# Output projection, first 1024 columns: seven products of block sums for six attention heads' K-tiles

## The chip, the cores and the metric

The kernel runs on one core of a Trainium2 chip. The metric is the device time of one execution in microseconds, the median of several runs. All times inside an execution are counted from the start of the profiled span. The profile page names the engines: PE is the matrix engine (PEld its weight load), DVE the vector engine, ACT the scalar engine, POOL the general engine that here only starts a few loads and does a few small operations, and SP the queue that starts the loads of weights.

## The reference

One decoder layer on 256 tokens of width 2048, in float32:

```python
h = rms_norm(x, ln_mix_pre[l])
proj = h @ w_in[l]
q, k, v, z, xbc, dt_raw = jnp.split(proj, splits, axis=-1)
attn = moba_attention(q.reshape(shp), k.reshape(shp), v.reshape(shp), rel_bias)
ssm = mamba2_mixer(z, xbc, dt_raw, ssm_conv_w[l], ...)
mixed = jnp.concatenate([attn, ssm], axis=-1) @ w_out[l]
x = x + rms_norm(mixed, ln_mix_post[l])
h = rms_norm(x, ln_ffn_pre[l])
u = causal_depthwise_conv(h @ w_ffn_up[l], ffn_conv_w[l], ffn_conv_b[l])
gate, up = jnp.split(u, [FFN_HIDDEN], axis=-1)
f = (jax.nn.gelu(gate, approximate=True) * up) @ w_ffn_down[l]
x = x + rms_norm(f, ln_ffn_post[l])
```

The change is in the line of `mixed`: a product of 256 x 2048 by 2048 x 2048. Attention has 8 heads of width 128, so one head is one K-tile of 128 rows of `w_out`; the other 8 K-tiles come from the state-space half.

## The kernel before

**Precision.** Each float32 operand is kept as two float32r summands, `hi` (rounded) and `lo` (the rest), and a product is three matmuls: hi by hi, hi by lo of the weights, lo by hi. The activations of the output projection lie in `mT`, sixteen K-tiles by two summands by 256 tokens.

**Weights.** All weights pass through one stream, the class `Weights`. A unit is 512 KB, 128 x 1024 floats. For a plain unit SP starts the load into `raw`, ACT writes `whi` and DVE writes `wlo`:

```python
self.load(out=raw[:, s], in_=self.units[i][0][:, s])          # L85, SP
nc.scalar.copy(hi[:, s], raw[:, s])                           # L86, ACT
nc.vector.tensor_tensor(lo[:, s], raw[:, s], f32(hi[:, s]),   # L87, DVE
                        op=ALU.subtract)
```

There are four buffers each of `raw`, `whi` and `wlo`. Loads go in order, and the load of a unit waits until the `wlo` of the unit four places earlier is written. After each unit that PE has used, `tick` fetches the next one and counts down the list of deferred work. `deepen` (after the mixer's buffers are given back) adds three buffers to `whi` and to `wlo`, none to `raw`, and lets the next three ticks fetch two units each.

**Pairs.** The down projection of the feed-forward half already has units of another kind, written `Q` in its orders (`FIVE`, `FOUR`): two units of weights (`same` and `other`) make four steps on PE. The third step's weights (`two`) and the fourth's (`more`) are sums that DVE forms from the two loaded ones (L141, L144, L145, into a tile `ts`). Each of the four gets its own `whi` (L137, ACT) and `wlo` (L146, DVE). PE multiplies them by block sums of the activations (`quad_operands`, L1075 to L1089) in `product` (L1095 to L1097): seven products for a 2 x 2 block of the result where plain units take eight. `quad_sums` (L1104 to L1108) adds them up.

**Output projection.** Its 2048 columns are four chunks of 512. A chunk has 8 units (two K-tiles by 512 columns each); a unit is 12 matmuls of 128 x 512: two token tiles, two K-tiles, three matmuls (L317 to L319, `rows_part`). Each chunk has two PSUM tiles `pa`, one for each token tile, from a pool of four, so chunk 2 takes over the two tiles of chunk 0. Chunks 0 and 1 are opened with the four units of the state-space half each, while the last attention heads are still being finished by deferred work on the same engines (`logits`, `transposed`, `values`). Then the mixer's buffers are given back, and POOL starts four loads of 1 MB for what follows: two halves of `xt`, `wpost` and `lnrow` (L821, L826, L829). ACT scales `wpost` once (L827). Then come the four attention units of chunk 0 and those of chunk 1, chunk 2 with eight units and chunk 3.

When a chunk is complete, `post` runs for each token tile: ACT sums the squares out of PSUM (L235), DVE multiplies by `wpost` into `mm` (L850) and that by `lnrow` (L842). With L850 done the PSUM tile is free. Six products of `xt` by `lnrow` (L845) are deferred by 9 to 14 ticks.

**Order.** The instructions of the engines are put in order by a scheduler with its own estimate of durations, when the program is built; on the chip each engine takes its instructions in that order, and an instruction whose input is late holds up those behind it on its engine.

Of the kernel before, what the change touches and what calls it, by code (L numbers as in the profile page):

```python
# [158 lines left out]


@with_exitstack
def decoder_layer(ctx, tc, x, xT, win, wdt, wout, wup, wdown, relb, vec, cols, mconv, fconv,
# [248 lines left out]
    with ExitStack() as mctx:  # L411
        mx = mctx.enter_context(tc.tile_pool(name="mx", bufs=1))
        mT = mx.tile([P, KT, 2, S], F32R, name="mT")

# [432 lines left out]
        def post(c):  # L847
            def fn(t, ps):
                square_sum(ss[0][t][:, c:c + 1], ps)
                nc.vector.tensor_tensor(mm[:, t, chunk(c)], ps, wpost[:, chunk(c)], op=ALU.mult)  # L850
# [221 lines left out]

    def quad_operands(k, cg, cu):
# [10 lines left out]
        nc.vector.tensor_tensor(v[:, 4:8:2], v[:, 0:2], v[:, 3::-3], op=ALU.subtract)  # L1084
        nc.vector.tensor_tensor(v[:, 5], v[:, 4], v[:, 1], op=ALU.subtract)
        nc.vector.tensor_tensor(v[:, 7], v[:, 2], v[:, 5], op=ALU.add)
        src, hi, lo = g8[0][:, P:], gx[:, j, 0, :], gx[:, j, 1, :]
        nc.scalar.copy(hi, src)
        nc.vector.tensor_tensor(lo, src, f32(hi), op=ALU.subtract)  # L1089
# [306 lines left out]
```

## Time and profile before

| what | value |
|---|---|
| median of 3 runs | 1097.23 us (1096.92 to 1097.73) |
| the profiled execution | 1097.02 us, span 1095.2 us |
| mean granted PE clock | 0.999 |
| PE, PEld, DVE, ACT, POOL busy | 1089.5, 936.1, 885.4, 622.8, 14.5 us |
| first matmul of the output projection | 277.41 us |
| first matmul of chunk 2 | 323.90 us |
| loads of `w_out` | 32 of 512 KB, median 4.0 us to landing |
| POOL's loads after the mixer | 4 of 1 MB, started from 297.24 to 298.89 us |

The busy shares are means over the layer. What the change touches lies between 277 and 324 us, and in that stretch each engine is read by itself: when a `whi` or a `wlo` is written, and when PE asks for it. In a timeline row the columns are start, duration, engine, line, operation, output from input, count, and in brackets the idle time before it and what ended it.

### The profile page before, as it was taken

The page shows a single profiled execution, that of the slowest core. Times are in us where ns is not written, and L with a number is a line of the kernel's source. Part 1 is how long each engine was busy: PE and PEld are TensorE (multiplying, and loading weights), DVE is VectorE, ACT ScalarE, POOL GpSimd, SP SyncE. Part 2 cuts the span into 40 slices and gives each one's busy share as a digit, 9 for nine tenths or more (in the row PEclk, how much of TensorE's full clock was granted, in tenths as well). Part 3 has the DMA queues.
Part 4 walks back from the last instruction along what each step waited for, and adds up shares of the span by engine and source line. Part 5 has one row for each costly group of instructions (what it writes and reads, how often), then busy time and mean ns, then how long its engine had stood idle before and what let it go on. Part 6 is the DMA issues. An engine that isn't in the chain of part 4 may idle for free.

```text
span 1095.2 us, 15949 instructions
## 1 busy us (share of the span) xinstructions
PE 1089.5 (99%) x5858; PEld 936.1 (85%) x5858; DVE 885.4 (81%) x1422; ACT 622.8 (57%) x945; POOL 14.5 (1%) x24
## 2 busy tenths in 40 slices
PE   9999999999999999999999999999999999999998
PEld 7888888888888998888888888888888888888887
DVE  6689976766568699888878999978888787888987
ACT  6666544644455486655555564646556555565552
POOL 0000000000000000000000000000000000000000
PEclk9999999999999999999999999999999999999999
DMA  9858544554687276656665476675566665656562
GB/s 308 301 174 269 191 154 152 177 180 166 182 320 252 76 254 212 208 183 192 190 191 191 135 232 190 215 245 186 187 189 193 189 192 193 189 178 217 185 219 88
DMA packets 61646, 217.59 MB, mean 199 GB/s; under 512 B 7104, under 2 KB 8912, under 8 KB 60928
## 3 DMA queue, kind: packets, MB, share of 16 engines
q1 hardware_dynamic: 59616, 207.53, 58.5%
q0 software_dynamic: 1664, 8.59, 2.1%
q8 instruction: 46, 0.75, 0.3%
q10 hardware_dynamic: 288, 0.46, 0.1%
q14 instruction: 32, 0.26, 0.1%
HBM read 214.44 MB, written 2.11 MB: 198 GB/s over the span
## 4 chain that ended last, share of the span: by engine, by line
PE 99%; DMA 0%; SPq 0%; ACT 0%; DVE 0%; issue 0%
PE pa L253 37%; PE pa L254 19%; PE pa L317 5%; PE pa L319 5%; PE pa L318 5%; PE ph L318 4%; PE ph L317 4%; PE ph L319 4%; PE pa L1096 1%; PE pa L1097 1%; PE pa L1095 1%; PE pab L253 1%; PE ph L1096 1%; PE ph L1097 1%; PE ph L1095 1%; PE pa L262 1%
## 5 line engine op out<-in xcount | busy, mean ns | idle before, releaser
L86 ACT CAST whi<-raw 128x1024 fp32r<-128x1024 f32 (+2 forms) x353 | 365.2, 1038 | 323.0 <-PE pa L253 186.6
L87 DVE TENSOR_TENSOR wlo<-raw,whi 128x1024 fp32r<-128x1024 f32 (+2 forms) x353 | 424.7, 1208 | 141.6 <-ACT whi L86 133.6
L253 PE MATMUL pa<-h,whi 128*128 128x512 f32 x1360 | 471.7, 394 | 0.0
L254 PE MATMUL pa<-h,wlo 128*128 128x256 f32 x1360 | 379.2, 279 | 0.0
L253 PEld LDWEIGHTS pa<-h,whi 128*128 128x128 f32 x1360 | 255.4, 188 | 57.5
L254 PEld LDWEIGHTS pa<-h,wlo 128*128 128x128 f32 x1360 | 255.3, 188 | 0.0
L253 PE MATMUL pa<-hT,whi 128*128 128x512 f32 x384 | 137.0, 398 | 0.0
L254 PE MATMUL pa<-hT,wlo 128*128 128x256 f32 x384 | 107.2, 280 | 0.0
L253 PEld LDWEIGHTS pa<-hT,whi 128*128 128x128 f32 x384 | 72.1, 188 | 15.8 <-issue 0.2
L1034 DVE SCALAR_TENSOR_TENSOR cfc<-cfu,fcv,cfc 128x255 f32<-128x255 f32 (+1 forms) x176 | 83.4, 479 | 2.1 <-ACT cfc L1032 0.6
L317 PE MATMUL ph<-whi,gT 128*128 128x512 f32 x190 | 73.9, 389 | 0.0
L319 PE MATMUL ph<-whi,gT 128*128 128x512 f32 x190 | 73.9, 389 | 0.0
L318 PE MATMUL ph<-wlo,gT 128*128 128x512 f32 x190 | 73.9, 389 | 0.0
L254 PEld LDWEIGHTS pa<-hT,wlo 128*128 128x128 f32 x384 | 72.2, 188 | 0.4 <-issue 0.2
L137 ACT CAST whi<-ts 128x1024 fp32r<-128x1024 f32 x36 | 37.3, 1049 | 31.3 <-DVE ts L145 16.8
L1032 ACT ACTIVATE cfc<-cfu,fcv 128x256 f32<-128x256 f32 x88 | 52.2, 598 | 3.7 <-DVE cfu L1031 3.7
L317 PE MATMUL pa<-whi,hT 128*128 128x512 f32 x128 | 51.1, 399 | 0.0
L317 PE MATMUL pa<-whi,mT 128*128 128x512 f32 x128 | 50.3, 393 | 0.0
L319 PE MATMUL pa<-whi,hT 128*128 128x512 f32 x128 | 50.1, 391 | 0.0
L318 PE MATMUL pa<-wlo,hT 128*128 128x512 f32 x128 | 50.0, 391 | 0.0
L318 PE MATMUL pa<-wlo,mT 128*128 128x512 f32 x128 | 50.0, 390 | 0.0
L319 PE MATMUL pa<-whi,mT 128*128 128x512 f32 x128 | 49.9, 390 | 0.0
(306 smaller groups left out, 1391.2 us busy)
## 6 DMA issues: line engine op xcount, KB each, us to landing
raw<-in_wup_dram SPq DMA_DIRECT2D x176, 512.0 KB, 3.5
raw<-in_wdown_dram SPq DMA_DIRECT2D x88, 512.0 KB, 3.9
raw<-in_win_dram SPq DMA_DIRECT2D x85, 512.0 KB, 3.6
...
xt<-in_x_dram POOLq DMA_DIRECT2D x2, 1024.0 KB, 7.2
...
```

Source lines behind the costliest of these rows:

```text
L86: nc.scalar.copy(hi[:, s], raw[:, s])
L87: return lambda: nc.vector.tensor_tensor(lo[:, s], raw[:, s], f32(hi[:, s]), op=ALU.subtract)
L137: nc.scalar.copy(hi[:, :n], raw[:, :n])
L253: nc.tensor.matmul(ps, w[0][:, s], both, start=(k == 0), stop=False)
L254: end[0] = nc.tensor.matmul(ps[:, c], w[1][:, s], hi, start=False, stop=(k == KT - 1)).ins
L317: nc.tensor.matmul(ps, a, w[0][:, s], start=(first and j == 0), stop=False)
L318: nc.tensor.matmul(ps, a, w[1][:, s], start=False, stop=False)
L319: end[0] = nc.tensor.matmul(ps, b, w[0][:, s], start=False, stop=(last and j == 1)).ins
L1032: nc.scalar.activation(c, u, AF.Identity, scale=wv[:, 2:3], bias=wv[:, 3:4])
L1034: nc.vector.scalar_tensor_tensor(c[:, sh:], u[:, :S - sh], wv[:, 2 - sh:3 - sh], c[:, sh:], op0=ALU.mult, op1=ALU.add)
L1095: nc.tensor.matmul(ps, a, w[0][:, s], start=first, stop=False)
L1096: nc.tensor.matmul(ps, a, w[1][:, s], start=False, stop=False)
```

## The change

Three of the four attention units of chunk 0 and the three of chunk 1 with the same K-tiles (heads 0 to 5) become three pairs; one pair covers two heads and both chunks. Heads 6 and 7 stay plain. The order of the first 1024 columns is the string `OUTER`: four units of chunk 0, two of chunk 1, and then, after the mixer's buffers are given back, pair, unit of chunk 1, pair, unit of chunk 1, pair, unit of chunk 0, unit of chunk 1.

- The weights' sums use the free half of `mm` instead of `ts` (class `Spare`).
- When a head's values come out of PSUM, ACT also copies them to `og`; after each second head DVE forms the block sums (`block_sums`) and ACT and DVE split the four new blocks into `oq`.
- A pair's seven products go to four PSUM tiles `pm7` of their own and to three of the four chunk tiles. After the third pair `first_sums` writes them into `mm`: one copy on ACT, four operations on DVE.
- `post` of chunks 0 and 1 now first adds PSUM to `mm` on DVE; the sum of squares and the product by `wpost` read `mm`. With that addition done the PSUM tile is free.
- The products of `xt` by `lnrow` are deferred by 17 to 22 ticks. The units of `w_out` stand in the new order in memory.
- In the feed-forward half the same operations as before are now called through the shared helpers.

```diff
+OUTER = "000011Q1Q1Q01"
+OQ = OUTER.count("Q")
...
+class Spare:
...
+    def tile(self, *args, **kwargs):
+        self.n += 1
+        return self.places[self.n % len(self.places)]
...
+    def block_sums(v):
...
+        nc.vector.tensor_tensor(v[:, 4:8:2], v[:, 0:2], v[:, 3::-3], op=ALU.subtract)
+        nc.vector.tensor_tensor(v[:, 5], v[:, 4], v[:, 1], op=ALU.subtract)
+        nc.vector.tensor_tensor(v[:, 7], v[:, 2], v[:, 5], op=ALU.add)
+
+    def split(hi, lo, src):
+
+        nc.scalar.copy(hi, src)
+        nc.vector.tensor_tensor(lo, src, f32(hi), op=ALU.subtract)
+
+    def product_of(ps, a, b, w, h, first, last):
+
+        s = chunk(h)
+        nc.tensor.matmul(ps, a, w[0][:, s], start=first, stop=False)
+        nc.tensor.matmul(ps, a, w[1][:, s], start=False, stop=False)
+        end[0] = nc.tensor.matmul(ps, b, w[0][:, s], start=False, stop=last).ins
+
+    def first_sums(f, p1, p6, p7, q5):
+
+        tt = nc.vector.tensor_tensor
+        nc.scalar.copy(f[0][0], p1)
+        tt(f[1][0], p6, f[0][0], op=ALU.add)
+        tt(f[0][1], p7, f[1][0], op=ALU.add)
+        tt(f[1][1], q5, f[0][1], op=ALU.subtract)
+        tt(f[1][0], q5, f[1][0], op=ALU.subtract)
...
+    def out_units():
+
+        found, at = [], 0
+        for what in OUTER:
+            if what == "Q":
+                found += [("same", wout[at]), ("other", wout[at + 1]), ("two",), ("more",)]
+                at += 2
+            else:
+                found += units(wout, at, 1)
+                at += 1
+        return found + units(wout, at, 16)
...
+                if h < 2 * OQ:
+                    out_operands(h, po[:, S - 1::-1])
...
+            def out_operands(h, a):
+
+                j, odd = divmod(h, 2)
+                if not odd:
+                    og[0] = ax.tile([P, 8 * P], F32, name="og", tag="og", bufs=1)
+                    nc.scalar.copy(blocks(og[0])[:, 1::-1], blocks(a))
+                    return
+                nc.scalar.copy(blocks(og[0])[:, 2:4], blocks(a))
+                block_sums(blocks(og[0]))
+                split(oq[:, j, 0, :], oq[:, j, 1, :], og[0][:, 4 * P:])
...
+            mm = pers.tile([P, NT, D], F32, name="mm", tag="mm", bufs=1)
+            ws.sums = Spare([mm[:, t, UE:] for t in range(NT)])
             lo, hi = range(8, KT, 2), range(0, 8, 2)
             first = [chunk_psums() for _ in range(2)]
-            for c in range(2):
-                rows_chunk(first[c], mT, lo, last=False)
+            taken = [list(lo) + list(hi[OQ:]) for _ in range(2)]
+            for what in OUTER[:6]:
+                c = int(what)
+                rows_step(first[c], mT, taken[c].pop(0), first=len(taken[c]) == 4 - OQ + 3)
...
             def fn(t, ps):
+                m = mm[:, t, chunk(c)]
+                if c < 2:
+                    nc.vector.tensor_tensor(m, ps, m, op=ALU.add)
+                    ps = m
                 square_sum(ss[0][t][:, c:c + 1], ps)
-                nc.vector.tensor_tensor(mm[:, t, chunk(c)], ps, wpost[:, chunk(c)], op=ALU.mult)
+                nc.vector.tensor_tensor(m, ps, wpost[:, chunk(c)], op=ALU.mult)
...
+        def out_pair():
...
+            once = [psum("pm7") for _ in range(4)]
+            p1, p7, q5, p6 = once
+            j = 0
+            for what in OUTER[6:]:
+                if what == "Q":
+                    for items in (((p1, 0, 0), (first[1][0], 6, 1)), ((first[0][0], 1, 0),),
+                                  ((q5, 3, 0), (p7, 5, 1)), ((p6, 4, 0), (first[0][1], 2, 1))):
+                        w = ws.take()
+                        for ps, block, h in items:
+                            mine = any(ps is z for z in once)
+                            out_product(ps, j, block, w, h, mine and j == 0,
+                                        mine and j == OQ - 1)
+                        tick()
+                    j += 1
+                    if j == OQ:
+                        first_sums([[mm[:, t, chunk(n)] for t in range(NT)] for n in range(2)],
+                                   p1, p6, p7, q5)
+                else:
+                    c = int(what)
+                    k = taken[c].pop(0)
+                    rows_step(first[c], mT, k, last=not taken[c],
+                              soon=None if taken[c] else post(c))
...
-            defer(9 + i, x_weighted, t, c)
-        for c in range(2):
-            rows_chunk(first[c], mT, hi, first=False, soon=post(c))
+            defer(17 + i, x_weighted, t, c)
+        out_pair()
```

The scheduler's order around it, at the places where PE's weights come from. First ACT, from the stretch in which POOL's four loads are under way to the end of the first two chunks. Before: the units 10 to 17 of `w_out` (`raw_2998` is unit 10, `raw_3016` unit 11, `raw_3067` unit 12, and so on).

```order
L86 CAST whi_3068<-raw_3067 128x1024
L86 CAST whi_2999<-raw_2998 128x1024
L86 CAST whi_3074<-raw_3073 128x1024
L86 CAST whi_3017<-raw_3016 128x1024
L86 CAST whi_3092<-raw_3091 128x1024
L86 CAST whi_3098<-raw_3097 128x1024
L86 CAST whi_3116<-raw_3115 128x1024
L827 ACTIVATE wpost_3038<-wpost_3038 128x2048
L86 CAST whi_3122<-raw_3121 128x1024
```

And now. `raw_3091` is load 11 (a plain unit of chunk 1), `raw_3105` and `raw_3123` are loads 12 and 13, the third pair's `same` and `other`; `raw_3153` and `raw_3165` are loads 14 and 15, the plain units behind that pair; `whi_3134` and `whi_3143` are the third pair's `two` and `more`, `pm7_3043` one of its products.

```order
L88 CAST whi_3092<-raw_3091 128x1024
L139 CAST whi_3103<-raw_3105 128x1024
L139 CAST whi_3121<-raw_3123 128x512
L88 CAST whi_3154<-raw_3153 128x1024
L912 ACTIVATE wpost_3026<-wpost_3026 128x2048
L139 CAST whi_3134<-mm_2862 128x1024
L88 CAST whi_3166<-raw_3165 128x1024
L387 COPY mm_2862<-pm7_3043 128x512
L139 CAST whi_3143<-mm_2862 128x1024
L88 CAST whi_3184<-raw_3183 128x1024
```

The weights of load 14 and the scaling of `wpost` now stand ahead of the third pair's `two`, which PE uses before load 14; load 15 and the copy stand ahead of `more`.

Second DVE, from the third pair's `two` to the operation that frees the PSUM tile of chunk 0's first token tile, which chunk 2 takes over (`pa_2863` in the rows of the change). Before, from the last `wlo` ahead of it (`raw_3121` is unit 17, two units into chunk 2):

```order
L87 TENSOR_TENSOR wlo_3099<-raw_3097,whi_3098 128x1024
L87 TENSOR_TENSOR wlo_3117<-raw_3115,whi_3116 128x1024
L845 TENSOR_TENSOR xl0_3044<-xt_3025,lnrow_3041 128x512
L87 TENSOR_TENSOR wlo_3123<-raw_3121,whi_3122 128x1024
L850 TENSOR_TENSOR mm_3024<-pa_2837,wpost_3038 128x512
L850 TENSOR_TENSOR mm_3024<-pa_2838,wpost_3038 128x512
```

And now (`raw_3183` is load 16, chunk 2's first unit; `raw_3204`, `raw_3216` and `raw_3228` are loads 18 to 20):

```order
L89 TENSOR_TENSOR wlo_3167<-raw_3165,whi_3166 128x1024
L148 TENSOR_TENSOR wlo_3144<-mm_2862,whi_3143 128x1024
L89 TENSOR_TENSOR wlo_3185<-raw_3183,whi_3184 128x1024
L89 TENSOR_TENSOR wlo_3197<-raw_3195,whi_3196 128x1024
L388 TENSOR_TENSOR mm_2862<-pm7_3046,mm_2862 128x512
L89 TENSOR_TENSOR wlo_3206<-raw_3204,whi_3205 128x1024
L389 TENSOR_TENSOR mm_2862<-pm7_3044,mm_2862 128x512
L89 TENSOR_TENSOR wlo_3218<-raw_3216,whi_3217 128x1024
L89 TENSOR_TENSOR wlo_3230<-raw_3228,whi_3229 128x1024
L390 TENSOR_TENSOR mm_2862<-pm7_3045,mm_2862 128x512
L391 TENSOR_TENSOR mm_2862<-pm7_3045,mm_2862 128x512
L936 TENSOR_TENSOR mm_2862<-pa_2863,mm_2862 128x512
```

Seven `wlo` of 1024 (the six of loads 15 to 20 and that of `more`) and the four sums of `first_sums` now stand between the third pair's `two` and the addition that frees chunk 2's first PSUM tile. Before, the tile was freed by L850 right behind the `wlo` of unit 17.

More of the change, by code (lines that the diff above doesn't have):

```diff
@@ L158, in take, with __init__ @@
         return self.ready.pop(0)
+class Spare:
+    def __init__(self, places):
+        self.places, self.n = places, 0
+    def tile(self, *args, **kwargs):
+        self.n += 1
+        return self.places[self.n % len(self.places)]
 @with_exitstack
@@ L336, in rows_chunk, with rows_step, blocks @@
                 done(t, pss[t])
+    def rows_step(pss, aT, k, first=False, last=False, soon=None):
+        w = ws.take()
+        for t in range(NT):
+            rows_part(pss[t], w, aT, k, t, first, last)
+        if soon:
+            for t in range(NT):
+                soon(t, pss[t])
+        tick()
+    def blocks(ap):
+        return ap.rearrange("p (b c) -> p b c", c=P)
+    def block_sums(v):
[17 more added lines that the diff above has]
+        tt(f[1][0], q5, f[1][0], op=ALU.subtract)
     def rows_to_tail(pss, aT, kts, first=True):
@@ L413, in decoder_layer @@
         mT = mx.tile([P, KT, 2, S], F32R, name="mT")
+        oq = mx.tile([P, OQ, 2, 4 * P], F32R, name="oq")
         with ExitStack() as actx:
@@ L1083, in quad_operands @@
         nc.vector.tensor_tensor(v[:, 2:4], blocks(cg), blocks(cu), op=ALU.mult)
[L1084 to L1089, printed above, removed]
-    def product(ps, j, block, w, h, first, last):
-        a, b = (gx[:, j, c, :][:, tok(block)] for c in range(2))
-        s = chunk(h)
-        nc.tensor.matmul(ps, a, w[0][:, s], start=first, stop=False)
-        nc.tensor.matmul(ps, a, w[1][:, s], start=False, stop=False)
-        end[0] = nc.tensor.matmul(ps, b, w[0][:, s], start=False, stop=last).ins
+        block_sums(v)
+        split(gx[:, j, 0, :], gx[:, j, 1, :], g8[0][:, P:])
+    def product(ps, j, block, w, h, first, last):
+        product_of(ps, *(gx[:, j, c, :][:, tok(block)] for c in range(2)), w, h, first, last)
     def quad_sums(half, c, p1, p6, p7, q5):
@@ L1103, in quad_sums @@
         if half == 0:
-            nc.scalar.copy(f[0][0], p1)
-            tt(f[1][0], p6, f[0][0], op=ALU.add)
-            tt(f[0][1], p7, f[1][0], op=ALU.add)
-            tt(f[1][1], q5, f[0][1], op=ALU.subtract)
-            tt(f[1][0], q5, f[1][0], op=ALU.subtract)
+            first_sums(f, p1, p6, p7, q5)
             return
@@ L1338 @@
     ssm, att = [4, 5, 6, 7], [0, 1, 2, 3]
-    wout = np.concatenate([o[0, ssm], o[1, ssm], o[0, att], o[1, att],
-                           o[2, ssm + att], o[3, ssm + att]])
+    head, quads = [], iter(att)
+    plain = [iter(ssm + att[OQ:]) for _ in range(2)]
+    for what in OUTER:
+        if what == "Q":
+            k = next(quads)
+            (b11, b21), (b12, b22) = (o[n, k].reshape(P, 2, 512).swapaxes(0, 1) for n in range(2))
+            head += [np.concatenate(z, axis=1) for z in ((b11, b22), (b21, b12))]
+        else:
+            head.append(o[int(what), next(plain[int(what)])])
+    wout = np.concatenate([np.stack(head), o[2, ssm + att], o[3, ssm + att]])
     up = cols(w_up).reshape(2, NF, 2, P, UE)
```

14 lines of the change are left out of this document (10 added, 4 removed).

## The prediction

> **What bounds the kernel now.** I read the page first (busy shares, the chain of work that ended last), then the stretch of the change in windows, and then the timelines of ACT, DVE and SP there.
>
> ```profile
> PE 1089.5 (99%) x5858; PEld 936.1 (85%) x5858; DVE 885.4 (81%) x1422; ACT 622.8 (57%) x945; POOL 14.5 (1%) x24
> PE 99%; DMA 0%; SPq 0%; ACT 0%; DVE 0%; issue 0%
> ```
>
> PE is the whole chain: a matmul less is time saved, if PE doesn't wait in its place. So the question is how early PE's weights are ready. The stretch in windows (columns: busy of PE, PEld, DVE, ACT and POOL with counts, granted clock, DMA share, GB/s):
>
> ```profile
> 303.00:307.00 4.00, 4.00 (x20) 3.30 (x19) 0.00 (x0) 0.15 (x1) 0.00 (x0) 1.00 1.04 431
> 307.00:311.00 4.00, 4.00 (x19) 3.12 (x18) 2.37 (x2) 2.24 (x3) 0.00 (x0) 1.00 1.00 417
> 311.00:315.00 4.00, 4.00 (x19) 3.29 (x18) 1.23 (x1) 0.66 (x1) 0.00 (x0) 1.00 1.01 408
> 315.00:319.00 4.00, 4.00 (x20) 3.30 (x19) 2.83 (x3) 3.74 (x3) 0.00 (x0) 1.00 0.61 224
> ```
>
> From 303 to 315 us the DMA engines are full, and DVE and ACT stand nearly still, waiting for weights; PE lives on what was prepared. The DMA view of 298 to 314 us says who fills the engines:
>
> ```profile
> q0 software_dynamic: 575, 4.19, 66.9%
> q1 hardware_dynamic: 553, 2.01, 31.0%
> lnrow<-in_vec_dram POOLq DMA_DIRECT2D x1, 1024.0 KB, 15.9
> ```
>
> POOL's four loads (4.19 MB) take two thirds, the weights one third. When three units of weights were asked for (SP), and when ACT got them:
>
> ```profile
> 298.42 0.33 SPq L85 DMA_DIRECT2D raw<-in_wout_dram  x1
> 301.77 0.33 SPq L85 DMA_DIRECT2D raw<-in_wout_dram  x1
> 302.91 0.33 SPq L85 DMA_DIRECT2D raw<-in_wout_dram  x1
> 306.85 2.00 ACT L86 CAST whi<-raw 128x1024 fp32r<-128x1024 f32 x2 [5.41 <-DMA raw<-in_wout_dram]
> 310.61 1.05 ACT L86 CAST whi<-raw 128x1024 fp32r<-128x1024 f32 x1 [1.76 <-DMA raw<-in_wout_dram]
> 315.04 1.05 ACT L86 CAST whi<-raw 128x1024 fp32r<-128x1024 f32 x1 [3.38 <-DMA raw<-in_wout_dram]
> 316.31 1.05 ACT L86 CAST whi<-raw 128x1024 fp32r<-128x1024 f32 x1 [0.22 <-DMA raw<-in_wout_dram]
> 317.27 1.91 ACT L827 ACTIVATE wpost<-wpost 128x2048 f32<-128x2048 f32 x1
> 319.09 1.03 ACT L86 CAST whi<-raw 128x1024 fp32r<-128x1024 f32 x1
> ```
>
> The first three loads that meet POOL's arrive at 306.8, 310.6 and 315.0, 8 to 12 us after they were asked for; the fourth is there at 316.3. PE in the same stretch:
>
> ```profile
> 296.42 0.48 PE L317 MATMUL pa<-whi,mT 128*128 128x512 f32 x1
> 299.24 0.39 PE L317 MATMUL pa<-whi,mT 128*128 128x512 f32 x1
> 310.12 0.39 PE L317 MATMUL pa<-whi,mT 128*128 128x512 f32 x1
> 310.36 0.50 PE L318 MATMUL pa<-wlo,mT 128*128 128x512 f32 x1
> 323.90 0.39 PE L317 MATMUL pa<-whi,mT 128*128 128x512 f32 x1
> ```
>
> 296.42 is the seventh unit, where the first pair will stand. 299.24 to 310.12 are 48 matmuls: 0.2267 us each. The matmul at 310.36 took 0.50 us: it waited for a `wlo`. So today's margin is used up once already, by about 0.1 us. 323.90 is chunk 2.
>
> **What is removed.** Three pairs of 21 matmuls replace 72 plain ones: 9 x 0.2267 = 2.04 us. With the 0.11 us at 310.36 and some rounding the most that can be gained is 2.3 us. Without a wait PE reaches the third pair's `two` 75 matmuls after 296.42, at 313.4 (two pairs of 21, two units of 12 and 9 of the third), and chunk 2 after 111, at 321.6.
>
> **What is added.** Each kind has a row in today's feed-forward pairs or beside it:
>
> ```profile
> L146 DVE TENSOR_TENSOR wlo<-ts,whi 128x1024 fp32r<-128x1024 f32 x36 | 43.6, 1222 | 7.4 <-ACT whi L137 7.2
> L141 DVE TENSOR_TENSOR ts<-raw 128x1024 f32<-128x1024 f32 x18 | 21.9, 1219 | 2.2 <-DMA raw<-in_wdown_dram 2.1
> L146 DVE TENSOR_TENSOR wlo<-raw,whi 128x512 fp32r<-128x512 f32 x18 | 12.3, 685 | 0.3 <-ACT whi L137 0.3
> L137 ACT CAST whi<-ts 128x1024 fp32r<-128x1024 f32 x36 | 37.3, 1049 | 31.3 <-DVE ts L145 16.8 <-DVE ts L141 8.7 <-PE ph L1097 3.0
> L1104 ACT COPY fa<-pa 128x512 f32<-128x512 f32 x2 | 1.2, 577 | 0.0
> 300.52 2.36 DVE L87 TENSOR_TENSOR wlo<-raw,whi 128x1024 fp32r<-128x1024 f32 x2 [1.79 <-ACT whi L86]
> 321.29 1.28 DVE L850 TENSOR_TENSOR mm<-pa,wpost 128x512 f32<-128x512 f32 x2
> ```
>
> Back to back DVE needs 2.36 / 2 = 1.18 us for 1024 elements and 1.28 / 2 = 0.64 for 512. A pair takes four operations of 1024 and three of 512, 6.6 us, where its two plain units took 2.4; PE uses a pair up in 21 x 0.2267 = 4.8 us. `first_sums` adds four of 512 and `post` four more. Of the block sums in the heads' part (per two heads one of 256, two of 128, one of 512 on DVE) I expect nothing: DVE waits there, as in the third of these rows, and PE's weights are ready four units ahead. If that cover were gone it would cost up to 0.43 + 2 x 0.28 + 0.69 = 1.7 us per two heads.
>
> ```profile
> L1084 DVE TENSOR_TENSOR ts<-ts 128x256 f32<-128x256 f32 x9 | 3.8, 426 | 0.2
> L1085 DVE TENSOR_TENSOR ts<-ts 128x128 f32<-128x128 f32 x9 | 2.6, 284 | 0.0
> 291.37 1.23 DVE L87 TENSOR_TENSOR wlo<-raw,whi 128x1024 fp32r<-128x1024 f32 x1 [1.24 <-ACT whi L86]
> ```
>
> **The path, step by step.** (1) Loads. SP asks for loads 12, 13 and 14 when DVE has freed their `raw` buffers. Load 12 follows the `wlo` of load 8, which stands behind the last head's values:
>
> ```profile
> 298.31 0.42 DVE L241 TENSOR_TENSOR mT<-pav,mT 128x256 fp32r<-128x256 f32 x1
> ```
>
> That gives about 299.9; loads 13 and 14 follow the second pair's sums, by the same operations about 302.4 and 304.2. This is 1.5, 0.6 and 1.3 us behind today's three and still ahead of their turn, so they land as those do, at 306.8, 310.6 and 315.0. The first two pairs and the plain units are prepared in time by the same adding up, with about 1 us to spare at the second pair's `more` (`wlo` at 306.4, asked for at 307.5).
>
> (2) The first wait. The third pair's `two` needs only loads 12 and 13, but in ACT's order its `whi` stands behind load 14 and the scaling of `wpost`. Taken from the rows' own spacing: load 14 at 315.04, 0.96 on (316.31 to 317.27) the scaling, 1.82 on (317.27 to 319.09) the `whi` of `two`, 1.05 for it: 318.9, instead of 313.4. PE waits 5.5 us. The second matmul needs the `wlo`, 1.22 later, at 320.1: 1.0 more. `more` needs load 15's `whi` (0.96), the copy (0.58) and its own (1.05), all in ACT's line: 321.4, where PE is ready at 321.2: 0.2. Behind that PE has 30 matmuls, 6.8 us, and is at chunk 2 at 328.2. If only this happened: 4.3 us late.
>
> (3) The second wait. Chunk 2 takes chunk 0's PSUM tile, free after the first L936. Between the `wlo` of `two` (320.1) and it DVE has seven operations of 1024 and four of 512: 7 x 1.18 + 4 x 0.64 = 10.8, and itself 0.68: 331.6. PE waits 3.4 us more. Queued behind L936 are the second tile's addition, 0.64 on, which PE asks for 1.36 later, and load 21, needed five units later: no further wait. Later DVE has room, as here, so nothing of it is given back or lost again:
>
> ```profile
> 341.73 1.23 DVE L87 TENSOR_TENSOR wlo<-raw,whi 128x1024 fp32r<-128x1024 f32 x1 [1.23 <-ACT whi L86]
> ```
>
> **Sum.** 331.6 - 323.9 = 7.7 us: the waits are 5.5 + 1.0 + 0.2 + 3.4 = 10.1, the gain 2.3, and 0.1 is rounding. Against the profiled execution: 1095.2 + 7.7 = 1102.9 of span, and with the 1.8 us around it (1097.02 - 1095.2) 1104.7; the median lies 0.2 above that execution, so 1104.9: **1105 us**.
>
> **Bounds.** The landing of load 14 has no row of its own. At the earliest it is today's second place, 310.6, at the latest the fourth, 316.2. At 310.6 the same adding up ends at about 329 (load 13 is then ACT's limit, and `more` still waits for load 15): +5.1; at 316.2 +8.9. I take the third place, since that is its place in the queue.
>
> **Rivals.** (a) *The other side: the stock covers it.* PE never waits, 2.0 to 2.3 us are gained, 1095.0. For it speaks that the feed-forward half runs such pairs, with DVE nearly full, without a wait of PE:
>
> ```profile
> 620.00:630.00 10.00, 10.00 (x46) 8.29 (x45) 9.94 (x14) 6.13 (x8) 0.00 (x0) 1.00 0.50 152
> ```
>
> There the DMA share is 0.50, here 1.0. It decides if load 14 lands before 309.5 (3.9 us, the way from landing to `whi` in step 2, before 313.4) and DVE is through 2 us earlier than (b) says. (b) *DVE's work alone.* If no load were late, DVE would still have, from the row at 294.10 on (today unit 8's `wlo`, then the first pair's `two`), 19 operations of 1024, 11 of 512 and one of 256 to L936's end:
>
> ```profile
> 294.10 1.23 DVE L87 TENSOR_TENSOR wlo<-raw,whi 128x1024 fp32r<-128x1024 f32 x1 [1.50 <-ACT whi L86]
> ```
>
> 19 x 1.18 + 11 x 0.64 + 0.42 = 29.9: chunk 2 at 324.0, where it starts today; 1097.3. (c) *The first wait alone.* If DVE got through the eleven operations of step 3 in the 8.1 us that PE needs from 320.1 to 328.2, chunk 2 would start then: +4.3, 1101.5. Against it: they take 10.8 by the rows, and DVE's order leaves none out. (d) *The clock falls.* When PE stops at the end of the span the granted clock goes down:
>
> ```profile
> 1088.00:1092.00 4.00, 3.03 (x20) 2.07 (x18) 3.19 (x10) 1.71 (x5) 0.00 (x0) 1.00 0.48 171
> 1092.00:1095.20 3.20, 0.00 (x0) 0.00 (x0) 0.00 (x0) 0.00 (x0) 0.00 (x0) 0.67 0.53 198
> ```
>
> A wait of 5.5 us can do that too. Half speed between 320 and 328 is hidden by up to 3.4 us under the second wait; if the clock is low after 331.6 for as long as one of the waits lasted (3.4 to 5.5 us), half of it is lost: 1.7 to 2.7 more, about 1107. [...] That the products aren't fewer can be left out: PE's order holds nine matmuls less.
>
> **How the numbers follow.** Forecast 0.64, its own range 1102.3 (load 14 in second place, 5.1 late) to 1106.1 (fourth place, 8.9 late); (a) 0.06, (b) 0.12, (c) 0.06, (d) 0.12. A measurement of this kernel can tell about 0.2%, 2.2 us, from no change. (a) lies on that border and is split; (b) is within it, with a part above: faster 0.03, same 0.12, slower 0.85. The range takes in (c) and (d) with about 2 us on either side of them and leaves out (a) and (b), 0.18 together: 1099.5 to 1109.
>
> **What would show it.** In the new profile: PE idle of 4 to 6 us near 313 with ACT's `whi` of `two` as its end; ACT's row of load 14 at about 315 with an idle time put down to the DMA, and `wpost` right behind it; a second idle of PE of 2 to 4 us at the start of chunk 2, ended by DVE L936; the start of chunk 2 7 to 8 us later than now, and equal spans from there on. I am wrong if load 14's cast comes before 311, or if PE is at chunk 2 before 324.

## The result and the profile after

| | time | |
|---|---|---|
| before | 1096.98 us (6 runs, 1096.61 to 1097.73) | |
| with the change | 1104.86 us (6 runs, 1104.73 to 1106.70) | ratio 1.0075, 95% interval 1.0062 to 1.0088 |

The change makes the layer 7.9 us slower; 1105.0 was forecast. The page of the changed kernel: busy shares, and the chain of work that ended last.

```profile
PE 1091.7 (99%) x5849; PEld 936.6 (85%) x5849; DVE 906.1 (82%) x1457; ACT 631.3 (57%) x961; POOL 14.0 (1%) x24
PE 95%; DVE 2%; DMA 1%; issue 1%; ACT 1%; POOL 0%; ACTq 0%; SPq 0%; DVEq 0%
```

There are nine matmuls less, as the change says. The second line is new: PE was 99% of the chain, and now 5% of it belongs to others. The same stretch in windows as before (busy of PE, PEld, DVE, ACT, POOL with counts, granted clock, DMA share, GB/s):

```profile
315.00:319.00 4.00, 1.23 (x3) 0.29 (x1) 2.97 (x4) 4.00 (x5) 0.00 (x0) 0.74 0.52 155
319.00:323.00 4.00, 3.62 (x9) 2.84 (x10) 3.83 (x4) 3.11 (x5) 0.00 (x0) 0.50 0.90 310
327.00:331.00 4.00, 2.66 (x12) 1.88 (x10) 3.60 (x5) 2.16 (x3) 0.00 (x0) 1.00 0.87 284
```

A full window holds 19 or 20 matmuls. From 315 to 319 there are three: PE waits, while ACT is busy for all of the 4 us. From 319 to 323 there are nine, although PE waits for 0.46 us only: the granted clock is 0.50. From 327 to 331 PE waits again, now with DVE busy. PE's instructions that waited, and the first of chunk 2:

```profile
314.70 0.50 PE L381 MATMUL pa<-wlo,mT 128*128 128x512 f32 x1 [0.63 <-DVE wlo L148]
318.13 0.79 PE L380 MATMUL pm<-whi,oq 128*128 128x512 f32 x1 [2.69 <-ACT whi L139]
319.38 0.80 PE L381 MATMUL pm<-wlo,oq 128*128 128x512 f32 x1 [0.46 <-DVE wlo L148]
331.62 0.47 PE L330 MATMUL pa<-whi,mT 128*128 128x512 f32 x1 [1.96 <-DVE mm L936]
```

318.13 is the third pair's `two`; 331.62 is chunk 2, which stood at 323.90. What ACT and DVE did ahead of these two:

```profile
309.10 1.05 ACT L139 CAST whi<-raw 128x1024 fp32r<-128x1024 f32 x1 [2.58 <-DMA raw<-in_wout_dram]
312.82 1.23 DVE L143 TENSOR_TENSOR mm<-raw 128x1024 f32<-128x1024 f32 x1 [1.40 <-DMA raw<-in_wout_dram]
314.28 1.05 ACT L88 CAST whi<-raw 128x1024 fp32r<-128x1024 f32 x1 [0.77 <-DMA raw<-in_wout_dram]
315.24 1.90 ACT L912 ACTIVATE wpost<-wpost 128x2048 f32<-128x2048 f32 x1
317.05 1.03 ACT L139 CAST whi<-mm 128x1024 fp32r<-128x1024 f32 x1
318.11 1.22 DVE L148 TENSOR_TENSOR wlo<-mm,whi 128x1024 fp32r<-128x1024 f32 x1 [0.91 <-ACT whi L139]
...
323.36 1.22 DVE L89 TENSOR_TENSOR wlo<-raw,whi 128x1024 fp32r<-128x1024 f32 x1 [0.52 <-ACT whi L88]
328.45 1.23 DVE L89 TENSOR_TENSOR wlo<-raw,whi 128x1024 fp32r<-128x1024 f32 x1 [0.40 <-ACT whi L88]
330.80 1.28 DVE L936 TENSOR_TENSOR mm<-pa,mm 128x512 f32<-128x512 f32 x2
```

309.10 is load 12, and the sum at 312.82 had waited for load 13. Then the forecast picture: load 14 late in ACT's line (314.28), `wpost` behind it, `two` behind that; and DVE at L936 only at 330.80.

Two more things are needed to read the runs. The first 60 us of the program shift by up to 0.6 us from run to run, so in what follows each matmul is compared with the same matmul of the kernel before (counted from the end, since nine are missing), and the shift at the 900th matmul (164.6 us, before any change) is taken off. And by that measure a part of the loss is far from the output projection: at 188.9 us the changed kernel falls 0.47 us behind, and keeps it. The first two heads' block sums stand 12 us ahead of that place:

```profile
177.12 0.42 DVE L368 TENSOR_TENSOR og<-og 128x256 f32<-128x256 f32 x1 [0.44 <-ACT og L870]
186.50 0.16 DVE L208 TENSOR_TENSOR rsq<-rsy 128x1 f32<-128x1 f32 x1
186.97 1.23 DVE L89 TENSOR_TENSOR wlo<-raw,whi 128x1024 fp32r<-128x1024 f32 x1
188.30 0.48 DVE L810 TENSOR_SCALAR xs<-xs,rsr 128x512 f32<-128x512 f32 x1
188.93 0.63 PE L817 MATMUL pyt<-cst,xs 128*128 128x128 f32 x4 [0.26 <-DVE xs L810]
```

The same operations in the kernel before (L195 is L208 there):

```profile
186.60 0.16 DVE L195 TENSOR_TENSOR rsq<-rsy 128x1 f32<-128x1 f32 x1
187.38 0.49 DVE L742 TENSOR_SCALAR xs<-xs,rsr 128x512 f32<-128x512 f32 x1
187.78 1.22 DVE L87 TENSOR_TENSOR wlo<-raw,whi 128x1024 fp32r<-128x1024 f32 x1
```

The state-space gate's `xs`, which PE's transposes L817 need at once, comes 0.92 us later from DVE. The work of the sums isn't what delays it: at L208 DVE is level with the kernel before (186.50 against 186.60). But with the sums in the program the scheduler has put a unit's `wlo` ahead of `xs`, which it followed before.

All runs by this measure (us later than the kernel before, each from its one profiled execution; "median" is over all executions; the label is that of the experiment):

| run | median | at 189 us | at chunk 2 | 48 matmuls on |
|---|---|---|---|---|
| the change | 1104.86 | 0.47 | 7.69 | 7.79 |
| pairs_first | 1099.67 | 0.47 | 2.79 | 2.79 |
| before_no_pool | 1096.92 | 0.00 | -0.19 | -0.19 |
| after_no_pool | 1101.65 | 0.47 | 2.55 | 4.27 |
| no_scaling | 1107.52 | 0.47 | 7.62 | 10.61 |
| other_banks | 1102.87 | 0.47 | 5.57 | 5.57 |
| no_pool_banks | 1095.83 | 0.47 | -1.47 | -1.47 |
| three_all | 1098.19 | 0.35 | 0.74 | 0.74 |
| two_all | 1096.92 | 0.35 | -0.44 | -0.44 |
| order_late | 1096.02 | 0.00 | -1.53 | -1.53 |
| three_late | 1096.83 | 0.00 | -0.47 | -0.47 |
| two_late | 1096.14 | 0.00 | -1.33 | -1.33 |
| order_kept | 1096.05 | 0.00 | -1.89 | -1.89 |

### The profile page after: what moved, and what is told of

Same layout as the page of the kernel before. It is cut to its first block, busy times and chain, and to the rows that moved or that the text cites. A ratio compares the mean times of both kernels' runs of the same rounds, so it can differ in the third digit from the quotient of the medians.

```text
span 1103.1 us, 15984 instructions
## 1 busy us (share of the span) xinstructions
PE 1091.7 (99%) x5849; PEld 936.6 (85%) x5849; DVE 906.1 (82%) x1457; ACT 631.3 (57%) x961; POOL 14.0 (1%) x24
## 4 chain that ended last, share of the span: by engine, by line
PE 95%; DVE 2%; DMA 1%; issue 1%; ACT 1%; POOL 0%; ACTq 0%; SPq 0%; DVEq 0%
PE pa L266 36%; PE pa L267 18%; PE ph L330 4%; PE ph L332 4%; PE ph L331 4%; PE pa L330 4%; PE pa L331 4%; PE pa L332 4%; PE pa L380 1%; PE pa L381 1%; PE pa L382 1%; PE pab L266 1%; DMA raw<-in_wout_dram 1%; PE ph L380 1%; PE ph L381 1%; PE ph L382 1%
## 5 line engine op out<-in xcount | busy, mean ns | idle before, releaser
L88 ACT CAST whi<-raw 128x1024 fp32r<-128x1024 f32 (+2 forms) x347 | 359.1, 1038 | 302.2 <-PE pa L266 182.4
L89 DVE TENSOR_TENSOR wlo<-raw,whi 128x1024 fp32r<-128x1024 f32 (+2 forms) x347 | 417.6, 1208 | 121.6 <-ACT whi L88 114.3
L139 ACT CAST whi<-raw 128x1024 fp32r<-128x1024 f32 (+1 forms) x42 | 34.9, 836 | 34.1 <-PE ph L332 13.8
L148 DVE TENSOR_TENSOR wlo<-ts,whi 128x1024 fp32r<-128x1024 f32 x36 | 43.7, 1222 | 8.9 <-ACT whi L139 8.7
L330 PE MATMUL pa<-whi,mT 128*128 128x512 f32 x104 | 41.2, 396 | 2.0 <-DVE mm L936 2.0
```

The lines of the kernel that those rows point to most:

```text
L89: return lambda: nc.vector.tensor_tensor(lo[:, s], raw[:, s], f32(hi[:, s]), op=ALU.subtract)
L139: nc.scalar.copy(hi[:, :n], raw[:, :n])
L148: return lambda: nc.vector.tensor_tensor(lo[:, :n], raw[:, :n], f32(hi[:, :n]), op=ALU.subtract)
L330: nc.tensor.matmul(ps, a, w[0][:, s], start=(first and j == 0), stop=False)
```

## The experiments

The theory going in: late loads make ACT late with the third pair's `two` (first wait), and DVE's queue then frees chunk 0's PSUM late (second wait). The rivals: DVE's work alone; the pairs cost it wherever they stand; the loads aren't the cause.

### The pairs ahead of the plain units (pairs_first)

```diff
-OUTER = "000011Q1Q1Q01"
+OUTER = "000011QQQ0111"
```

> The change, but with the three pairs ahead of the four plain units (order 000011 Q Q Q 0 1 1 1), so that the pairs use loads 6 to 11, which are asked for before POOL's four loads start. Theory 'late loads': no wait of PE for a load of a pair; the pairs' DVE work (7 operations of 1024, 6 of 512 from 299.1 us on) ends at about 310.8 where PE asks at 310.1, a wait of 0.7; chunk 2 between 322.9 and 325.6 us, the time 1096.2 to 1098.9. Rival 'DVE's work alone': the sum of DVE's work up to the first L936 is the same as in the changed kernel and 0.6 more (one product of xt), so chunk 2 is at about 324.6, 1098. Rival 'pairs cost it wherever they stand': chunk 2 at 331.6, 1105.

Measured: 1099.67 us, ratio 1.0023 (1.0013 to 1.0033). Neither "wherever they stand" (1105) nor any of the sums. Chunk 2 starts without a wait for L936, but 2.79 us late. PE's longest wait there and ACT's line, and then the windows of the wait and behind it:

```profile
309.38 1.92 ACT L912 ACTIVATE wpost<-wpost 128x2048 f32<-128x2048 f32 x1 [1.01 <-DMA wpost<-in_vec_dram]
311.20 1.03 ACT L139 CAST whi<-mm 128x1024 fp32r<-128x1024 f32 x1
312.28 0.50 PE L380 MATMUL pm<-whi,oq 128*128 128x512 f32 x1 [1.75 <-ACT whi L139]
```
```profile
310.25:313.66 3.41, 1.45 (x6) 0.61 (x5) 1.40 (x2) 2.92 (x3) 0.00 (x0) 1.00 1.00 404
313.66:317.07 3.41, 3.41 (x10) 2.67 (x10) 3.25 (x4) 3.04 (x3) 0.00 (x0) 0.50 0.77 227
```

No load of a pair is late, but POOL's are: the scaling of `wpost` waits for its own 1 MB and holds up the last `more` behind it on ACT. The wait of 1.75 us is followed by 3.4 us at half clock, which the theory hadn't counted here. It cost little: L936 starts at 325.19 us in this trace, and in the changed kernel chunk 2 followed the start of L936 by 0.82 us, so PE could have begun chunk 2 at 326.0 at the earliest instead of 326.83. Of the nine executions five have a mean clock of 0.999 or 1.000, where 3.4 us at one half would leave 0.998 at most; their median is 1099.57 us, that of the other four 1099.73.

### The change without POOL's loads (before_no_pool, after_no_pool)

```diff
-            aux(out=xt[:, t, :], in_=x[0, tok(t), :])
+            for _ in range(1):
+                nc.gpsimd.memset(xt[:, t, :], 0.5)
...
-        aux(out=wpost, in_=row_bcast(V_MIXPOST, D))
+        for _ in range(1):
+            nc.gpsimd.memset(wpost, 0.5)
...
-        aux(out=lnrow, in_=row_bcast(V_FFNPRE, D))
+        for _ in range(1):
+            nc.gpsimd.memset(lnrow, 0.5)
...
-            nc.vector.tensor_tensor(xl[t][c], xt[:, t, chunk(c)], lnrow[:, chunk(c)], op=ALU.mult)
+            pass
```

> The kernel before, with POOL's four loads of 1 MB (two of xt, wpost, lnrow) replaced by fills with a constant on POOL, and the six products of xt by lnrow left out: the result is that of other inputs. All theories: loads of weights land 3 to 5 us after they are asked for; the 0.11 us wait at 310.36 is gone, chunk 2 at 323.8, the time within 0.3 us of the kernel before plus what the six missing products are worth, which stand off the path: 1096.5 to 1097.3.

> The changed kernel with the same four loads replaced and the same six products left out; the order of PE is that of the changed kernel, that of DVE up to the first L936 too but for two neighbours that change places, and ACT scales wpost earlier. Theory 'late loads start it': the first wait is gone, DVE's work alone decides (rival b of the prediction): chunk 2 at about 324.0 to 324.5, the time 1097 to 1097.7, 0 to 0.7 above the kernel before without these loads. If DVE has room enough without late loads: chunk 2 at 322.1 (321.6 and 0.5 from the heads' part), 1095.5. If the loads aren't the cause: chunk 2 stays at 331.6, 1104.9.

Measured: 1096.92 (ratio to before 0.9999, 0.9989 to 1.0008) and 1101.65 (1.0044, 1.0029 to 1.0059). The first wait is gone; so the loads do start it, with the scaling of `wpost`, which stands earlier in ACT's order here (the next experiment takes the scaling away alone, and a wait stays). But 4.7 us of loss stay where 0 to 0.7 were expected. All of PE's wait is one:

```profile
326.12 0.47 PE L330 MATMUL pa<-whi,mT 128*128 128x512 f32 x1 [3.83 <-DVE mm L941]
```

(L941 is L936 of the changed kernel.) DVE's queue from the `wlo` with which rival (b) began its sum, with the idle times in it:

```profile
294.25 1.23 DVE L148 TENSOR_TENSOR wlo<-mm,whi 128x1024 fp32r<-128x1024 f32 x1 [2.47 <-ACT whi L139]
297.31 1.23 DVE L148 TENSOR_TENSOR wlo<-mm,whi 128x1024 fp32r<-128x1024 f32 x1 [0.57 <-ACT whi L139]
305.26 1.22 DVE L148 TENSOR_TENSOR wlo<-mm,whi 128x1024 fp32r<-128x1024 f32 x1 [1.18 <-ACT whi L139]
318.36 1.23 DVE L89 TENSOR_TENSOR wlo<-raw,whi 128x1024 fp32r<-128x1024 f32 x1 [0.98 <-ACT whi L88]
325.30 1.28 DVE L941 TENSOR_TENSOR mm<-pa,mm 128x512 f32<-128x512 f32 x2
```

From 294.25 to the end of the first addition (325.30 + 0.64) are 31.7 us: 29.0 of work, where the prediction had added up 29.9, and 2.7 of idle time, which it had left out. So even with every load early DVE frees the PSUM tile 3.8 us after PE wants it. And behind that wait 1.7 us more are lost (2.55 to 4.27 in the table), at half clock:

```profile
320.37:323.78 3.41, 1.93 (x9) 1.27 (x7) 3.41 (x4) 1.88 (x2) 0.00 (x0) 1.00 0.75 226
323.78:327.19 3.41, 1.06 (x5) 0.93 (x6) 3.41 (x6) 1.60 (x2) 0.00 (x0) 1.00 0.93 333
327.19:330.61 3.42, 3.42 (x10) 2.64 (x9) 2.73 (x5) 1.83 (x5) 0.00 (x0) 0.50 0.71 242
```

### ACT's line without the scaling (no_scaling)

```diff
-        nc.scalar.mul(wpost, wpost, -0.5)
```

> The changed kernel without the scaling of wpost by -0.5 on ACT (the result has another sign and size there). In ACT's order the whi of the third pair's two then stands right behind load 14's. Theory 'ACT's line': PE's first wait falls by 1.8 us, from 2.7 to about 0.9, and as DVE's eleven operations follow from there, chunk 2 comes 1.2 to 1.9 us earlier, 329.7 to 330.4: 1103.0 to 1103.7. Rival 'the second wait doesn't hang on the first' (DVE has its own late input): chunk 2 stays at 331.6, the second wait grows by what the first loses, 1104.9.

Measured: 1107.52 (1.0092, 1.0077 to 1.0107), 2.7 us slower than the change, where both theories had it faster or the same.

```profile
315.89 0.50 PE L380 MATMUL pm<-whi,oq 128*128 128x512 f32 x1 [1.94 <-ACT whi L139]
331.07 0.77 PE L330 MATMUL pa<-whi,mT 128*128 128x512 f32 x1 [3.91 <-DVE mm L935]
```
```profile
327.02:330.43 3.41, 0.14 (x1) 0.00 (x0) 3.20 (x5) 2.66 (x3) 0.00 (x0) 1.00 0.91 298
330.43:333.84 3.41, 2.77 (x7) 2.22 (x8) 3.41 (x6) 1.72 (x5) 0.00 (x0) 0.50 0.67 225
```

The rows say that `two` comes 2.24 us earlier (315.89 against 318.13); 0.48 of that is the shift of the first 60 us between the two executions, and the 1.76 that remain are the 1.8 of "ACT's line". PE's idle time at `two` falls only from 2.69 to 1.94, since PE is there about 1.0 us earlier too: the wait for load 13 is gone. But L936 (here L935) comes only 0.08 earlier, with the same shift taken off: one `wlo` and one sum more stand behind `two` in DVE's order of this build, 1.8 us of work, and the idle time among them is the same (0.87, 0.92 in the change). So the rival had the second wait right: chunk 2 stays where it was, and the wait grows (1.96 to 3.91). New is what follows: PE is busy for 0.14 us of the window ahead, the clock falls to one half from 330.43 to 337.25, and 3.0 us are lost behind chunk 2's start. That is rival (d) of the prediction, in a kernel that only leaves work out. The four executions differ widely, from 1104.89 to 1108.52 us: the lowest is as fast as the change. Whether its clock fell less there, no kept trace shows.

### Chunk 2 in other PSUM tiles (other_banks, no_pool_banks)

The tiles of two of the once-summed products are free before chunk 0's. Chunk 2 takes those; nothing else changes ahead of it.

```diff
-            p1, p7, q5, p6 = once
+            p1, p6, p7, q5 = once
...
-        rows_chunk(chunk_psums(), mT, both, soon=post(2))
+        rows_chunk([psum("pc2") for _ in range(NT)], mT, both, soon=post(2))
```

> The changed kernel, but chunk 2 takes the PSUM tiles of two of the once-summed products (p1, freed by ACT's copy at 319.5, and p6, freed by the first DVE addition at 325.2) in place of chunk 0's, which L936 frees at 331.4. Theory 'L936 makes the second wait': chunk 2 starts when PE is ready, at 329.7, 1.96 us earlier; 1102.9. Rival 'DVE is late anyway' (the wait moves to a weight of chunk 2 or to chunk 3): 1104.9, with a new wait of about 2 us behind 330.

> The changed kernel without POOL's four loads and without the six products of xt by lnrow (result of other inputs), and with chunk 2 in the once-summed products' PSUM tiles. Without the tiles' change PE waited 3.8 us at chunk 2 and ran about 1.7 us slower right behind it at a granted clock of 0.65. Theory 'two waits and the clock': both the wait and the slow stretch go, chunk 2 at 322.3, the time 1101.65 - 3.8 - 1.7 = 1096.1. If the slow stretch isn't the wait's doing: 1097.8. If DVE's total decides at a later place: 1101.6.

Measured: 1102.87 (1.0055, 1.0039 to 1.0071), forecast 1102.9; and 1095.83 (0.9990, 0.9981 to 0.9999), forecast 1096.1. In both PE has no wait at chunk 2 or behind it, so L936 makes the second wait, and PE loses nothing in its place later. In no_pool_banks PE waits nowhere between 280 and 360 us, its clock is 1.00 throughout, and the change pays: 1.47 us (1.28 against before_no_pool), which is 2.04 + 0.11 less the 0.47 of the heads and 0.2 of small steps.

### Versions that might beat both (three_all, two_all, order_late, three_late, two_late, order_kept)

Four edits together: the pairs first; the factor -0.5 in the product of `post`; chunk 2's other tiles; the first block sums put off by seven units.

```diff
-        nc.scalar.mul(wpost, wpost, -0.5)
...
-                nc.vector.tensor_tensor(m, ps, wpost[:, chunk(c)], op=ALU.mult)
+                nc.vector.scalar_tensor_tensor(m, ps, -0.5, wpost[:, chunk(c)], op0=ALU.mult,
+                                               op1=ALU.mult)
...
-                block_sums(blocks(og[0]))
-                split(oq[:, j, 0, :], oq[:, j, 1, :], og[0][:, 4 * P:])
+                if j:
+                    out_blocks(j, og[0])
+                else:
+                    defer(7, out_blocks, j, og[0])
```

> Four edits together, each against one wait found so far: pairs ahead of the plain units; the factor -0.5 of wpost in the product of post, so that ACT has no scaling in its line (it waited for POOL's load and held up the last pair's more by 1.3 us); chunk 2 in the once-summed products' tiles; the first two heads' block sums seven units later. Theory: PE waits 0.4 to 0.9 us at the third pair's more (DVE's sums end at 309.9, ACT's whi 1.05 on, PE ready at about 310.1 to 310.5), nothing at chunk 2 and nothing at 188; no slow stretch; chunk 2 at 322.2 to 322.7, the time 1095.4 to 1095.9, faster than before by 1.1 to 1.6. Rival 'DVE's total decides at a later place': a wait of 2 to 3 us behind 322, the clock down, 1099 or more.

> The same four edits with two pairs in place of three (heads 0 to 3; six matmuls less, 1.36 us): DVE and ACT have 4.2 and 2.1 us less to do. Theory: PE waits nowhere, chunk 2 at 323.9 - 1.36 - 0.1 = 322.4, the time 1095.6. Rival 'each pair costs PE more than it saves, by the loads or DVE': slower than three_all's gain by more than the missing 0.68, at 1097 or above.

Measured: 1098.19 (1.0010, 1.0001 to 1.0020) and 1096.92 (1.0001, 0.9992 to 1.0010); 1095.4 to 1095.9 and 1095.6 were forecast. In three_all the wait for `more` is what was said, but there are two more for plain units whose loads are late, which the forecast left out:

```profile
310.66 0.50 PE L380 MATMUL pm<-whi,oq 128*128 128x512 f32 x1 [0.54 <-ACT whi L139]
311.61 0.50 PE L330 MATMUL pa<-whi,mT 128*128 128x512 f32 x1 [0.21 <-ACT whi L88]
313.94 0.50 PE L330 MATMUL pa<-whi,mT 128*128 128x512 f32 x1 [0.60 <-ACT whi L88]
```
```profile
309.79:313.21 3.42, 2.67 (x10) 1.34 (x8) 2.36 (x2) 2.13 (x3) 0.00 (x0) 1.00 1.00 408
```

The edit at the heads took off 0.12 of the 0.47 only: the scheduler put the sums back to 176.94 us, where their input is ready. The second fence is the window of 3.41 us around these waits, as the last section reads them: PE was busy for 2.67 us of it, and the clock was 1.00 in it and behind it. With two pairs the projection gains 0.44, and then 0.8 is lost at 675 us, in the feed-forward half; two_late below loses 0.9 there. PE waits 0.53 and 0.58 us in that place for DVE to write `fa`; why two pairs change it was not tried.

So the next three hold back half of POOL's bytes: `xt` is loaded behind a small POOL operation that reads a column which the last of `first_sums` writes. And the first block sums are tied to data, with a one-column copy from the third head's values.

```diff
-        for t in range(NT):
-            aux(out=xt[:, t, :], in_=x[0, tok(t), :])
...
+                    if j == 1:
+                        nc.scalar.copy(og[0][:, 4 * P:4 * P + 1], a[:, :1])
+                        out_blocks(0, og[0])
...
         out_pair()
+        for t in range(NT):
+            nc.gpsimd.tensor_tensor(xt[:, t, :1], mm[:, 0, 512:513], mhalf[:, :1], op=ALU.mult)
+            aux(out=xt[:, t, :], in_=x[0, tok(t), :])
...
-            defer(17 + i, x_weighted, t, c)
+            defer(4 + i, x_weighted, t, c)
```

> The changed kernel in its own order of pairs, with every found cause taken away and a right result: xt's two loads (2 of POOL's 4 MB) held back by a small POOL operation that reads the last of the first sums, so that they start at about 320 instead of 297; the factor -0.5 in post's product; chunk 2 in the once-summed products' tiles; the first block sums tied to the third head's values. Theory: wpost and lnrow are through by about 306, loads 12 to 14 are no longer late, PE waits for nothing over 0.5 us; chunk 2 at 321.7 to 322.3, the time 1095.0 to 1095.6, 1.5 to 2 us faster than before. Rival 'the xt loads only collide later': a new wait of 1 to 3 us between 322 and 340 with the clock down behind it, 1097 to 1100. Rival 'two loads are enough to be late': a wait near 311 to 314, 1097 or more.

> The same edits with the three pairs first. Theory: the 1.1 us of waits for the loads of the plain units (311 to 313) go, the wait of about 0.7 for the third pair's more (DVE's 11.6 us of work from 299.1 on) stays: chunk 2 at 322.4 to 322.8, 1095.6 to 1096.0, a little slower than the changed kernel's own order. Rivals as there.

> The same edits with two pairs first. Theory: no wait, six matmuls less: chunk 2 at 322.5, 1095.6 to 1095.8. If xt's loads collide later: 1097 or more, as with three pairs.

Measured: 1096.02 (0.9989, 0.9981 to 0.9998), 1096.83 (0.9998, 0.9989 to 1.0007) and 1096.14 (0.9992, 0.9983 to 1.0000). The 0.47 us at the heads is gone, which shows that it came from where the first sums stood; `xs` is ahead of the `wlo` again. In the medians the change's own order is 0.8 us ahead of the three pairs first, as forecast; 0.1 from the two pairs is less than the executions differ. It gains 1.53 at chunk 2, where 1.6 to 2.2 were forecast; all three are 0.3 to 0.8 us above their forecasts. The loads of `xt` don't start at about 320 either. The column that POOL reads is written over by chunk 1's product with `wpost` (L944), and in order_late it is this that POOL waits for; the loads start at 336.97:

```profile
335.69 1.34 POOL L1030 TENSOR_TENSOR xt<-mm,mhalf 128x1 f32<-128x1 f32 x2 [37.16 <-DVE mm L944]
```

Against what was expected of it, order_late doesn't give the layer's result, nor do three_late and two_late: one of the products of `xt` comes behind the product that writes over the row it reads. The amount of work is the same. The last version has the six products in their right place.

```diff
-            defer(4 + i, x_weighted, t, c)
+            defer(1 + i, x_weighted, t, c)
```

> The same as order_late, but the six products of xt by lnrow come one to six units into chunk 2 in place of four to nine; in order_late, three_late and two_late one of them came behind the product that writes over the row it reads, so that a part of the result there was another (the work was the same). The order of PE, ACT and SP is unchanged. Theory: the same time as order_late's, 1095.7 to 1096.3, 0.8 to 1.4 us faster than before, with one wait of about 0.5 us at the third pair's two. Rival 'xt comes too late for the earlier products': DVE waits for xt's load in front of weights of chunk 2, a new wait of PE of 1 us or more behind 330, 1097 or more.

Measured: 1096.05 us against 1096.97, ratio 0.9991 (0.9982 to 1.0000). At chunk 2 it is 1.89 us ahead, nearly the whole gain. Then the rival happens in small:

```profile
342.66 1.29 DVE L935 TENSOR_TENSOR xl<-xt,lnrow 128x512 f32<-128x512 f32 x2 [0.76 <-DMA xt<-in_x_dram]
346.50 1.06 ACT L88 CAST whi<-raw 128x1024 fp32r<-128x1024 f32 x1 [6.96 <-DMA raw<-in_wout_dram]
357.08 0.50 PE L331 MATMUL pa<-wlo,mT 128*128 128x512 f32 x1 [0.40 <-DVE wlo L89]
358.95 0.49 PE L331 MATMUL pa<-wlo,mT 128*128 128x512 f32 x1 [0.20 <-DVE esb L225]
```

DVE waits for `xt`, ACT waits much longer for a load of weights, and 1.2 us are lost again by the end of chunk 3. order_late has the same wait of ACT (6.37 us) and loses nothing there; by 352 us it has begun four of the products, order_kept six. This version beats the change by 8.8 us, and the kernel before by 0.9 in the medians; the interval just reaches 1.

## Why the prediction was right, point by point

**The forecast**, 1105.0, and its two waits came out: PE idle at the third pair's `two`, ended by ACT's `whi`; PE idle at chunk 2, ended by L936; chunk 2 at 331.62 where 331.6 was said. Part of that closeness is luck: in point 3 two errors of 0.8 and 0.92 us cancel. Of the signs, the idle time at `two` is 2.69 us where 4 to 6 were named, and that at chunk 2 1.96 where 2 to 4 were; beside these two stand the waits of 0.63 and 0.46 us, the heads' 0.47 and about 2 us of slow clock.

**(1) Loads.** Two of the first three were later than taken over from before (load 12 at 309.1 instead of 306.8, load 13 at about 312.8 instead of 310.6), and load 14 was earlier, 314.28 instead of 315.04. The first two pairs were in time, as said. Load 13's lateness made a wait of its own (0.63, at 314.70) that the prediction doesn't have; it lies inside the time that `two` would have taken anyway.

**(2) The first wait.** From `two`'s own place, 313.9 (the predicted 313.4 and the 0.47 of the heads), to 318.13 are 4.2 us; 5.5 were said. The difference is load 14 (0.76) and the heads. The spacing from load 14 to `two` (0.96, then 1.81) is as taken from the rows before, and the 1.0 us for the `wlo` was 1.02 (319.38 less 318.13, less one step of 0.23).

**(3) The second wait** was 1.96 instead of 3.4. DVE had `two`'s `wlo` 0.8 earlier than said and lost 0.92 in two idle times that the sum of eleven operations leaves out, so L936 stood where it was forecast. PE was there 1.3 us later than forecast, at 329.5 instead of 328.2, in spite of its earlier start: its clock was at 0.50 until 323.74.

**The gain** of 2.04 us from nine matmuls less is real: no_pool_banks shows it.

**Heads' block sums: "I expect nothing"** was wrong, 0.47 us. DVE had the room that was assumed, as L208 at 186.50 shows. What the prediction left out is that a program with the sums in it gets another order: a `wlo` now stands ahead of the gate's `xs`, on which PE's next transposes wait.

**Rival (b), DVE's work alone, is the step that failed.** It gave 1097.3 for a kernel without late loads; that kernel takes 1101.65. The sum of DVE's work was good (29.0 against 29.9). Left out were DVE's idle times (2.7 us: its waits for ACT of 0.57, 1.18 and 0.98 us, each of which moved the end); and the half clock behind PE's wait (1.7 us). So the prediction put nearly all of the loss down to the late loads, and of 7.8 us they are 3.5 (7.79 - 4.27). The PSUM tile that L936 frees is worth 5.7 without them (4.27 + 1.47) and 2.2 with them (7.79 - 5.57): the first wait covers part of what the second would cost, and the other way round.

**Rival (d), the clock**, happened, in the form called hidden: 0.50 from 316.92 to 323.74, and about 2 us of it vanish under the second wait. Behind the second wait nothing covers it: there the half clock cost 3.0 us in no_scaling's trace and 1.7 in after_no_pool's. In pairs_first it came ahead of chunk 2 and cost at most 0.8. (a) and (c) didn't happen.

## What to carry to other kernels

Where one operation late in an in-order queue frees a buffer of the bottleneck engine, add up that queue's work with its waits, not its work alone (in after_no_pool 29.0 us of work and 2.7 of waits), and look first for another buffer: giving chunk 2 other PSUM tiles took off 2.2 us with the late loads and 5.7 without them, and cost PE no new wait. A change on one engine can also reorder another: look at the new order where nothing was meant to change. Before work is moved into a stretch, look at the loads that are started there for later: what is needed 20 us on can wait, though not too long (order_kept gives back 1.2 of its 1.89 us when `xt` comes). An operation that waits for a 1 MB load in ACT's line holds up what stands behind it: in pairs_first the scaling of `wpost` waited 1.01 us for its load, and PE 1.75 us for the `whi` behind it. Two waits of PE cost more than their length, in clock: 1.7 us more behind 3.83 in after_no_pool, 3.0 more behind 3.91 in no_scaling.

## What the runs showed of the clock

The trace records the granted clock as stretches, and all that lie inside these programs are multiples of 3.41 us: 0.5 for 3.41 us in pairs_first and after_no_pool, 6.83 in the changed kernel, 3.41 and 6.83 in no_scaling; and in the changed kernel full clock for 310.61 us (91 times 3.413) from the first record, at 6.30 us, to the first fall. Each trace is read here in windows of one such step. They lie differently in each: the first record is at 4.21 us in the trace of the kernel before and at 6.30 in that of the changed kernel. Three windows of the changed kernel, then one of before_no_pool and one of order_kept, both at the end of the program:

```profile
313.51:316.92 3.41, 1.24 (x3) 0.48 (x3) 3.29 (x5) 2.64 (x3) 0.00 (x0) 1.00 0.54 179
327.15:330.57 3.42, 2.51 (x12) 1.74 (x10) 3.02 (x4) 2.10 (x2) 0.00 (x0) 1.00 0.89 280
330.57:333.98 3.41, 2.36 (x10) 1.99 (x11) 3.41 (x6) 2.40 (x5) 0.00 (x0) 1.00 0.72 257
1089.35:1092.76 3.41, 1.65 (x9) 0.92 (x7) 1.92 (x4) 1.26 (x4) 0.00 (x0) 1.00 0.57 203
1088.88:1092.30 3.42, 1.79 (x10) 1.04 (x8) 2.05 (x4) 1.40 (x4) 0.00 (x0) 1.00 0.55 196
```

In these traces the clock was 0.50 behind the windows at full clock with PE busy for 1.24 and 1.65 us (the first and the fourth of these rows), 1.50 in the kernel before, 0.14 in no_scaling, 1.45 in pairs_first and 1.06 in after_no_pool; it was still 1.00 behind those with 1.79, 2.36 and 2.51 (the others here), 1.93 in after_no_pool and 2.67 in three_all. The count of matmuls doesn't tell the two apart: nine stand in the window with 1.65 and in that with 1.93. In no_scaling the clock was full again behind a slow window with 3.04 us busy, at 316.77, and not behind one with 2.77, at 330.43. The second wait of the changed kernel, 1.96 us, is split at 330.57 between two windows with 2.51 and 2.36 us busy, and the clock stayed at 1.00; the 1.75 us of pairs_first lie whole in one window of its profiled execution, with 1.45 us busy, and the clock behind it was 0.50. By their mean clock five of the nine executions of pairs_first have no such stretch; that the windows lay differently to the wait in these is an estimate, from the different places of the first record above. The busy time is the profile's own; what makes the chip lower the clock, no run shows.
